# Pacing the modulation sums of a two-layer diffusion trunk by two running clocks instead of fixed rates

## The chip, the cores and the metric

The kernel runs on one core of one Trainium2 chip. The time is device microseconds (us) of that core for one execution, the median of several runs. The engines are TensorE (PE; its weight loads are listed apart as PEld), VectorE (DVE), ScalarE (ACT), GpSimd (POOL) and SyncE (SP), which here only issues DMAs.

## What is computed

Two transformer layers, for 128 context rows and 256 latent rows that share all weights. Each layer starts from an adaLN modulation, one row vector for the context and one for the latents:

```
def _adaln(cond, w_mod, b_mod):
    m = jax.nn.silu(cond) @ w_mod + b_mod
    return jnp.split(m, 3, axis=-1)          # shift, scale, gate
h = _rmsnorm(y, norm_g) * (1.0 + scale) + shift
y = y + gate * mixer(h @ w_in) @ w_out
```

Layer 0's mixer is a gated linear recurrence (HGRN2) beside a grouped-query attention; layer 1's is a windowed attention. `w_mod` is 2048 x 6144 in each layer, all in float32. The change touches only when the parts of `silu(cond) @ w_mod` that are needed later are computed.

## The kernel before

**The matrix work.** All 384 rows stay on the chip. The large products (`h @ w_in`, `@ w_out`) run on PE in the fp32r type with three products each: a weight tile `raw` is split by ACT into `whi` (L328) and by DVE into the difference `wlo` (L330), and the activations stand split as `hh`, `hl`. `group` (L333) makes 512 columns of one product in eight **steps** of two 128-row weight tiles (512 KB): a step is 18 matmuls of 512 columns when rows are the output's partitions, or 24 of 384 columns when weights are. A group holds three or four of four PSUM buffers; the next group can take a buffer only after it was read out.

**The start stage.** Shift and scale of layer 0 are needed at once; `start_mod` makes them on PE while `start_group` (L688 to L690) multiplies the first six groups with the rows of the activations that are ready. It has 54 steps. I number the steps of the whole kernel 0 to 269: 0 to 53 are the start stage, then 27 groups of eight follow, 54 to 93 for the recurrence's value and the attention's inputs, 94 to 125 for gates, 126 to 157 for layer 0's output projection (four groups), 158 to 237 for layer 1's inputs, 238 to 269 for its output projection.

**The later sums.** Eight parts of the modulation are made beside that: four of layer 1's shift and scale (`mod_part`, in the order 16, 24, 0, 8) and four pairs of gate blocks (`mod_gates`: for layer 0's output groups 0 and 1, then 2 and 3; the same for layer 1). Each part reads 16 tiles of 512 KB, `mraw`, from the SP queue (L231) and sums them on DVE in `mod_acc`: two instructions of 1024 elements per tile (L244 for the first tile, L246 for the other fifteen). There is one `acc` buffer. A `mod_part` ends with matmuls against ones on PE (L256), a `mod_gates` with a split (ACT L285, DVE L287), matmuls against ones (L288, L289) and an addition of the bias (DVE L290); these free `acc` for the next part. `finish((layer, g))` after an output group makes the rest of the sum that its gate needs; the read-out of the group's PSUM (L1047) multiplies by that gate, so it waits for it.

**The order.** Each part is a Python generator, cut at its `yield`s into units: one that issues the first loads, sixteen of one tile each, and the ends. `step()` (L84) advances the recurrence and the attention by one piece; then `pump()` (L308) adds the rate `pace[1]` to a credit and calls `unit()` once for each whole credit. A piece that yields a weight takes `WEIGHT` times that from the credit (L90). Rates are 0.6 units per step in the start stage, 1.3 up to step 117, 0.9 up to 157, then 0.6. Where code stands sets its priority; the framework's scheduler places instructions on the engines by priority and readiness as it estimates them, so an instruction of low priority can come out earlier than its place in the code. The pieces of weights carry a raised priority (`tc.high_priority(BOOST)`).

Of the kernel before, what the change touches and what calls it, by code (L numbers as in the profile page):

```python
# [8 lines left out]
F32R = mybir.dt.float32r  # L9
# [5 lines left out]
P = 128  # L15
# [3 lines left out]
EPS = 1e-6  # L19
NEG = -1e30  # L20
BOOST = 100000
RATE = 1.3
RATE0 = 0.6
RAWB = 4
HIB = 3
# [3 lines left out]
PB = 2  # L29
EVY = 1  # L30
SRAW = 3
RATE1 = 0.9
WEIGHT = 0.25
RATE2 = 0.6
RATE3 = 0.6
MRAWB = 3
# [6 lines left out]

@with_exitstack
def trunk_kernel(ctx: ExitStack, tc: tile.TileContext, I, O):
    nc = tc.nc
    PSUM = bass.MemoryType.PSUM

    cpool = ctx.enter_context(tc.tile_pool(name="cpool", bufs=1))
# [27 lines left out]
    queue, due, pace = [], [], [0.0, 0.0]  # L77
# [6 lines left out]
    def step():  # L84
        if due:
            for f in due.pop(0):
                f()
        while queue:
            try:
                pace[0] -= WEIGHT * (next(queue[0]) or 0)  # L90
                return
            except StopIteration:
                queue.pop(0)
# [204 lines left out]
    def unit():  # L298
        while now or rows or mods:
            if not now:  # L300
                now.append((rows or mods).pop(0))
            try:
                next(now[0])
                return
            except StopIteration:
                now.pop()

    def pump():  # L308
        pace[0] += pace[1]
        while pace[0] >= 1.0:  # L310
            unit()
            pace[0] -= 1.0

# [62 lines left out]
    def group_a(w, c0, hq, after=None):  # L376
        return group(w, c0, hq, True, after)
# [266 lines left out]
    for g in range(4):  # L644
        x = xs[g]
# [24 lines left out]
    def pairs(k0, k1):  # L670

        out = []
        while k0 < k1:
            out.append((k0, min(2, k1 - k0, 4 - k0 % 4)))
            k0 += out[-1][1]
        return out
# [61 lines left out]
    for i, (k0, k1) in enumerate(phases):  # L738
# [4 lines left out]
        n = len(first) * len(pairs(k0, k1))  # L743
# [159 lines left out]

    pace[1] = RATE
    queue.append(hgrn_prep(0))
# [68 lines left out]
    def gate_heads(ps, o):  # L974
        gs = []
        for h in range(4):
            G = mpool.tile([P, 512], F32, tag="t2", bufs=T2B, name=nm("gt"))[:, 0:T]
            gate_fm(ps[h][:, 0:T], G)
            nc.vector.tensor_tensor(out=o[:, h], in0=o[:, h], in1=G, op=ALU.mult)
# [10 lines left out]
    ready0[0] = True  # L990
    pace[1] = RATE1
    gate_heads(group_a(W0, 7168, h0, after0), oB[1])
# [35 lines left out]
    for i, (c0, n) in enumerate(COLS):  # L1028
        g, o = c0 // 512, c0 % 512
        last = i == len(COLS) - 1  # L1030
        if o == 0:
            x = load_x("CD"[g % 2], g, nc.gpsimd)
# [102 lines left out]
    for c0, n in COLS:  # L1135
# [9 lines left out]
        for b in range(3):  # L1145
            for h in range(0, n, half):
                y = y4[:, b, o + h:o + h + half]
                t = mpool.tile([P, 512], F32, tag="t2", bufs=T2B, name=nm("t2"))[:, 0:half]
# [62 lines left out]
```

## Time and profile before

| | |
|---|---|
| median of 3 runs | 1369.67 us (1367.2 to 1371.61) |
| the profiled execution | 1371.0 us, of which the span from first to last instruction is 1369.1 us |
| mean granted TensorE clock | 0.994 |
| PE, PEld busy | 97%, 82% |
| DVE, ACT, POOL busy | 74%, 47%, 6% |

The busy share of DVE is uneven: in 40 slices of the span it is between 4 and 9 tenths. The profile is read by stages: which engine a stage waits for, and for how long PE stands still in it.

### The profile page before, as it was taken

How to read it: one execution, taken by the hardware profiler on the slowest of the kernel's cores; microseconds unless marked ns; L12 is line 12 of the kernel's file. 1: busy time of each engine (PE TensorE's matmuls, PEld its weight loads, DVE VectorE, ACT ScalarE, POOL GpSimd, SP SyncE). 2: the span in 40 equal slices, each digit the busy share in tenths (PEclk: the TensorE clock that was granted, in tenths of full speed). 3: DMA queues.
4: the chain of work that ended last, by engine and by line, in shares of the span. 5: the costliest groups of instructions: out<-in, count | busy, mean ns of one | idle time of the engine just before them, and what ended most of it. 6: DMA issues, size and time to landing. Idle time of an engine off the chain costs nothing.

```text
span 1369.1 us, 19104 instructions
## 1 busy us (share of the span) xinstructions
PE 1325.7 (97%) x7093; PEld 1126.7 (82%) x7093; DVE 1016.5 (74%) x1602; ACT 650.0 (47%) x1299; POOL 76.9 (6%) x84
## 2 busy tenths in 40 slices
PE   5899998999999999999999999999999999999998
PEld 4677777997888888688987787888888999998877
DVE  6588557998996799699498658994656664489734
ACT  3532233477554534566443336444766763352221
POOL 1000000000010022010000000200000101000000
PEclk9999999999999999999999999999999999999999
DMA  9999898745653367468458744784332335457642
GB/s 280 302 336 329 273 300 293 245 131 184 209 174 119 108 204 225 156 216 260 139 182 282 243 143 133 221 293 124 93 93 78 103 118 166 132 174 249 220 146 77
DMA packets 138317, 265.42 MB, mean 194 GB/s; under 512 B 8944, under 2 KB 46768, under 8 KB 138224
## 3 DMA queue, kind: packets, MB, share of 16 engines
q1 hardware_dynamic: 132592, 246.52, 55.6%
q0 software_dynamic: 5376, 17.60, 4.4%
q8 instruction: 56, 0.92, 0.3%
q14 instruction: 37, 0.30, 0.1%
q10 hardware_dynamic: 256, 0.08, 0.0%
HBM read 256.04 MB, written 8.13 MB: 193 GB/s over the span
## 4 chain that ended last, share of the span: by engine, by line
PE 70%; DVE 6%; ACT 1%; issue 1%; DMA 1%; POOL 0%; DVEq 0%; POOLq 0%
PE mm L354 59%; PE px L546 3%; DVE acc L246 2%; DVE wlo L330 2%; PE px L606 1%; PE px L623 1%; PE px L569 1%; PE px L861 1%; DMA mraw<-in_l_w_mod_dram 1%; PE px L864 1%; PE px L536 0%; PE px L878 0%; PE px L396 0%; PE px L868 0%; PE px L894 0%
## 5 line engine op out<-in xcount | busy, mean ns | idle before, releaser
L328 ACT CAST whi<-raw 128x1024 fp32r<-128x1024 f32 (+1 forms) x270 | 278.3, 1032 | 516.9 <-PE mm L354 394.6
L330 DVE TENSOR_TENSOR wlo<-raw,whi 128x1024 fp32r<-128x1024 f32 (+1 forms) x270 | 322.8, 1196 | 207.7 <-PE mm L354 161.2
L354 PE MATMUL mm<-whi,hh 128*128 128x512 f32 x1008 | 399.4, 397 | 2.0 <-DVE tF L639 1.7
L354 PE MATMUL mm<-wlo,hh 128*128 128x512 f32 x1008 | 391.6, 391 | 2.8 <-DVE wlo L330 2.8
L354 PE MATMUL mm<-whi,hl 128*128 128x512 f32 x1008 | 393.4, 391 | 0.6 <-DVE hl L1023 0.4
L246 DVE SCALAR_TENSOR_TENSOR acc<-mraw,csil,acc 128x1024 f32<-128x1024 f32 x240 | 299.4, 1277 | 13.0 <-DMA mraw<-in_l_w_mod_dram 13.0
L354 PEld LDWEIGHTS mm<-whi,hh 128*128 128x128 f32 x1008 | 189.4, 188 | 42.7 <-DVE tF L639 2.1
L354 PEld LDWEIGHTS mm<-wlo,hh 128*128 128x128 f32 x1008 | 189.3, 188 | 42.7 <-DVE wlo L330 5.6
L354 PEld LDWEIGHTS mm<-whi,hl 128*128 128x128 f32 x1008 | 189.3, 188 | 41.0 <-DVE hl L1023 0.8
L688 PE MATMUL mm<-hh,whi 128*128 128x384 f32 x384 | 132.9, 352 | 11.6 <-ACT whi L328 5.7
L354 PE MATMUL mm<-hh,whi 128*128 128x384 f32 x384 | 131.4, 342 | 0.0
L689 PE MATMUL mm<-hl,whi 128*128 128x384 f32 x384 | 131.2, 342 | 0.1
L354 PE MATMUL mm<-hh,wlo 128*128 128x384 f32 x384 | 129.3, 337 | 0.0
L354 PE MATMUL mm<-hl,whi 128*128 128x384 f32 x384 | 128.9, 336 | 0.0
L690 PE MATMUL mm<-hh,wlo 128*128 128x384 f32 x384 | 125.5, 341 | 2.2 <-DVE wlo L330 2.1
L688 PEld LDWEIGHTS mm<-hh,whi 128*128 128x128 f32 x384 | 73.6, 193 | 26.4 <-ACT whi L328 8.7
L690 PEld LDWEIGHTS mm<-hh,wlo 128*128 128x128 f32 x384 | 72.8, 191 | 5.4 <-DVE wlo L330 4.1
L689 PEld LDWEIGHTS mm<-hl,whi 128*128 128x128 f32 x384 | 73.7, 192 | 0.9 <-DVE hl L430 0.4
L354 PEld LDWEIGHTS mm<-hh,whi 128*128 128x128 f32 x384 | 72.1, 188 | 1.5 <-DVE tM L639 0.5
L354 PEld LDWEIGHTS mm<-hl,whi 128*128 128x128 f32 x384 | 72.2, 188 | 0.9
L354 PEld LDWEIGHTS mm<-hh,wlo 128*128 128x128 f32 x384 | 72.1, 188 | 0.6 <-issue 0.2
L581 ACT ACTIVATE p<-px,nb,rs 128x384 f32<-128x384 f32 (+1 forms) x72 | 42.4, 595 | 11.9 <-DVE nb L579 8.2
(450 smaller groups left out, 1395.7 us busy)
## 6 DMA issues: line engine op xcount, KB each, us to landing
raw<-in_l_w_in_dram SPq DMA_DIRECT2D x194, 512.0 KB, 3.9
mraw<-in_l_w_mod_dram SPq DMA_DIRECT2D x192, 512.0 KB, 5.1
raw<-in_l_w_out_dram SPq DMA_DIRECT2D x64, 512.0 KB, 4.5
raw<-in_l_w_in_dram SPq DMA_DIRECT2D x12, 256.0 KB, 7.4
tK<-in_l_b_mod_dram POOLq DMA_DIRECT2D x6, 256.0 KB, 6.0
y1d<-tA POOLq DMA_DIRECT2D x2, 768.0 KB, 7.3
tD<-y1d POOLq DMA_DIRECT2D x2, 768.0 KB, 6.5
tL<-y1d POOLq DMA_DIRECT2D x2, 768.0 KB, 6.5
```

The lines of the kernel that those rows point to most:

```text
L246: nc.vector.scalar_tensor_tensor(out=acc[:, c], in0=raw, scalar=s, in1=acc[:, c], op0=ALU.mult, op1=ALU.add)
L328: nc.scalar.copy(hi, raw)
L330: nc.vector.tensor_tensor(out=lo, in0=raw, in1=hi.bitcast(F32), op=ALU.subtract)
L354: nc.tensor.matmul(ps[c], lhsT=a, rhs=b, start=(kt == 0 and i == 0), stop=(kt + nk == KT and i == len(ops) - 1))
L546: nc.tensor.matmul(out, lhsT=a, rhs=b, start=(i == 0), stop=(i == len(ops) - 1))
L569: nc.tensor.matmul(s[:, 0:n], lhsT=qT[b][:, hc], rhs=kT[:, g, 0:n], start=True, stop=True)
L581: nc.scalar.activation(p[:, j], ss[j], AF.Exp, bias=nb[:, j:j + 1], scale=rs[:, i + j:i + j + 1], accum_out=sm[:, j:j + 1])
L606: nc.tensor.transpose(pp[:, k * P:k * P + P], p[:, j, k * P:k * P + P], ident)
L623: nc.tensor.matmul(o, lhsT=vs[kb][:, gc], rhs=ptt[0][:, j], start=(j == 0), stop=(j == len(ks) - 1))
L688: nc.tensor.matmul(ps[c][:, 0:T], lhsT=wh, rhs=hh[:, kq], start=(kt + k == k0), stop=False)
L689: nc.tensor.matmul(ps[c][:, 0:T], lhsT=wh, rhs=hl[:, kq], start=False, stop=False)
L690: nc.tensor.matmul(ps[c][:, 0:T], lhsT=wl, rhs=hh[:, kq], start=False, stop=(kt + k == k1 - 1))
```

## The change

The tracing code gets two clocks, in estimated us: `t` grows with each instruction that is issued to TensorE, `v` with each to VectorE, by three formulas. They exist only while the program is traced; on the chip no instruction is added or removed. `pump()` now makes a unit only where the credit allows it and `v` plus 2.7 is not above `t`; before that, `v` is raised to at least `t` minus 6. The credit is capped, the rates 1.3 and 0.9 become 2.0, the rates of the start stage and of layer 1 stay 0.6, and the weights that the pieces yield are no longer used.

```
-RATE = 1.3
+RATE = 2.0
-RATE1 = 0.9
-WEIGHT = 0.25
+RATE1 = 2.0
+BANK = 6.0
+UNIT = 2.7
...
+    clock = {"t": 0.0, "v": 0.0}
...
+    def cost_t(name, out, *a, lhsT=None, rhs=None, **k):
+        if rhs is None:
+            return 0.11
+        if lhsT.dtype == F32R:
+            return 0.013 + free(rhs) / 2400
+        return 4 * free(rhs) / 2400 * free(lhsT) / P
+
+    def cost_v(name, *a, **k):
+        aps = [x for x in (*a, *k.values()) if hasattr(x, "shape")]
+        n = max(free(x) for x in aps[:2])
+        return 0.12 + n / 1900 if name in ("tensor_copy", "tensor_scalar", "memset") else 0.17 + n / 950
...
             try:
-                pace[0] -= WEIGHT * (next(queue[0]) or 0)
+                next(queue[0])
                 return
...
     def pump():
-        pace[0] += pace[1]
-        while pace[0] >= 1.0:
+
+        pace[0] = min(pace[0] + pace[1], 2.0 + pace[1])
+        clock["v"] = max(clock["v"], clock["t"] - BANK)
+        while pace[0] >= 1.0 and clock["v"] + UNIT <= clock["t"]:
             unit()
             pace[0] -= 1.0
```

What is left out is a wrapper, `Counted`, that adds the cost to the clock and passes each call on to the engine, and `free`, the number of elements of one partition.

## Rows read from the trace of the kernel before

**Rows 1.** The page's part 1: busy us, share of the span, instructions.

```profile
PE 1325.7 (97%) x7093; PEld 1126.7 (82%) x7093; DVE 1016.5 (74%) x1602; ACT 650.0 (47%) x1299; POOL 76.9 (6%) x84
```

**Rows 2.** Windows: us, busy PE, PEld, DVE, ACT, POOL (x instructions), clock, DMA share, GB/s.

```profile
0.00:40.00 40.00, 25.02 (x187) 19.47 (x187) 23.96 (x54) 18.68 (x47) 3.59 (x10) 0.91 0.94 293
...
768.00:800.00 32.00, 32.00 (x142) 25.89 (x141) 13.70 (x16) 10.31 (x14) 0.00 (x0) 1.00 0.56 181
...
1240.00:1280.00 40.00, 40.00 (x179) 33.11 (x178) 39.50 (x37) 10.56 (x10) 0.75 (x1) 1.00 0.86 288
```

**Rows 3.** Groups by line, DVE: busy us, mean ns, idle before and its releasers.

```profile
L330 DVE TENSOR_TENSOR wlo<-raw,whi 128x1024 fp32r<-128x1024 f32 (+1 forms) x270 | 322.8, 1196 | 207.7 <-PE mm L354 161.2 <-ACT whi L328 22.4 <-issue 19.5
L246 DVE SCALAR_TENSOR_TENSOR acc<-mraw,csil,acc 128x1024 f32<-128x1024 f32 x240 | 299.4, 1277 | 13.0 <-DMA mraw<-in_l_w_mod_dram 13.0
```

**Rows 4.** Windows of line L256 alone, the ones matmuls: PE and PEld busy.

```profile
180.00:190.00 10.00, 1.04 (x8) 0.26 (x8) 1.00 1.03 352
315.00:325.00 10.00, 1.06 (x8) 0.16 (x8) 1.00 0.31 103
475.00:485.00 10.00, 1.06 (x8) 0.16 (x8) 1.00 0.24 68
575.00:585.00 10.00, 1.07 (x8) 0.16 (x8) 1.00 0.40 105
```

**Rows 5.** Windows of line L289 alone, the gates' second matmul against ones.

```profile
690.00:700.00 10.00, 1.23 (x3) 0.56 (x3) 1.00 0.37 119
```

**Rows 6.** Windows of line L246 alone, the sums: DVE busy us and instructions.

```profile
480.00:550.00 70.00, 34.19 (x28) 1.00 0.72 219
...
839.00:920.00 81.00, 36.93 (x30) 1.00 0.70 227
920.00:1200.00 280.00, 0.00 (x0) 1.00 0.39 115
```

**Rows 7.** All engines' windows in the start stage.

```profile
205.00:210.00 5.00, 5.00 (x40) 4.17 (x39) 1.35 (x2) 1.05 (x1) 0.00 (x0) 1.00 0.97 341
...
225.00:230.00 5.00, 5.00 (x21) 5.00 (x20) 3.99 (x4) 1.51 (x2) 0.00 (x0) 0.65 0.70 222
230.00:235.00 5.00, 5.00 (x31) 5.00 (x30) 3.99 (x6) 1.46 (x2) 0.00 (x0) 1.00 0.90 320
```

**Rows 8.** Timeline of SP, 185 to 211 us: start, us, issue (first and last).

```profile
185.00 0.50 SPq L231 DMA_DIRECT2D mraw<-in_l_w_mod_dram  x1
...
210.83 0.46 SPq L231 DMA_DIRECT2D mraw<-in_l_w_mod_dram  x1
```

**Rows 9.** Timeline of ACT and PE at 223 us, [idle before <-releaser].

```profile
223.07 1.04 ACT L328 CAST whi<-raw 128x1024 fp32r<-128x1024 f32 x1 [3.75 <-DMA raw<-in_l_w_in_dram]
224.17 0.69 PE L688 MATMUL mm<-hh,whi 128*128 128x384 f32 x1 [4.77 <-ACT whi L328]
```

**Rows 10.** Timeline of PE at 553 us.

```profile
553.14 0.50 PE L354 MATMUL mm<-whi,hh 128*128 128x512 f32 x1 [1.66 <-DVE tF L639]
```

**Rows 11.** Timeline of DVE and PE, 739 to 742 us.

```profile
739.55 1.28 DVE L246 SCALAR_TENSOR_TENSOR acc<-mraw,csil,acc 128x1024 f32<-128x1024 f32 x1 [4.99 <-DMA mraw<-in_l_w_mod_dram]
...
742.03 0.50 PE L354 MATMUL mm<-wlo,hh 128*128 128x512 f32 x1 [2.08 <-DVE wlo L330]
```

**Rows 12.** Timeline of DVE in layer 0's output projection.

```profile
700.41 0.75 DVE L244 TENSOR_SCALAR acc<-mraw,csil 128x1024 f32<-128x1024 f32 x1
...
722.09 0.69 DVE L1047 TENSOR_TENSOR tA<-mm,tK 128x512 f32<-128x512 f32 x1
...
727.37 4.86 DVE L246 SCALAR_TENSOR_TENSOR acc<-mraw,csil,acc 128x1024 f32<-128x1024 f32 x4
...
766.66 1.27 DVE L246 SCALAR_TENSOR_TENSOR acc<-mraw,csil,acc 128x1024 f32<-128x1024 f32 x1
...
796.64 0.68 DVE L1047 TENSOR_TENSOR tA<-mm,tK 128x512 f32<-128x512 f32 x1
...
800.32 0.68 DVE L287 TENSOR_TENSOR alo<-acc,ahi 128x512 fp32r<-128x512 f32 x1
```

More of the change, by code (lines that the diff above doesn't have):

```diff
@@ L45, in trunk_kernel, with free, __init__, __getattr__ @@
 def trunk_kernel(ctx: ExitStack, tc: tile.TileContext, I, O):
-    nc = tc.nc
+    clock = {"t": 0.0, "v": 0.0}
+    def free(ap):
+        n = 1
+        for d in ap.shape[1:]:
+            n *= d
+        return n
+    def cost_t(name, out, *a, lhsT=None, rhs=None, **k):
[8 more added lines that the diff above has]
+        return 0.12 + n / 1900 if name in ("tensor_copy", "tensor_scalar", "memset") else 0.17 + n / 950
+    class Counted:
+        def __init__(self, engine, key, cost):
+            self.engine, self.key, self.cost = engine, key, cost
+        def __getattr__(self, name):
+            f = getattr(self.engine, name)
+            def counted(*a, **k):
+                clock[self.key] += self.cost(name, *a, **k)
+                return f(*a, **k)
+            return counted
+    class Core:
+        vector, tensor = Counted(tc.nc.vector, "v", cost_v), Counted(tc.nc.tensor, "t", cost_t)
+        def __getattr__(self, name):
+            return getattr(tc.nc, name)
+    nc = Core()
     PSUM = bass.MemoryType.PSUM
```

## The prediction

> **What bounds the kernel now.** Part 1 of the page comes first: PE is busy for 1325.7 us of the span of 1369.1, DVE for 74% [rows 1]. Only 43.4 us have no matmul in flight, 15 of them in the first 40 us [rows 2], among the first loads and transposes, and the windows then show whether a busy PE still hides anything. In 1240 to 1280 us, with PE busy throughout, 179 matmuls of 512 columns run, one per 0.223 us [rows 2]; nothing in the change makes these faster. So a change that only moves DVE work can win no more than what PE stands still or crawls. The question is where PE waits for DVE, or for a DMA that a sum's load held up, and whether the change moves a sum away from there.
>
> The weight loads say something else at first sight: PEld is busy only 82% of the span [rows 1]. The Trainium skill ("Perfetto Trace Analysis", section "Identifying the Most-Contended Engine") holds that matmul busy time tells little about headroom and that weight-load busy time is the measure; by it 1369.1 - 1126.7 = 242 us would be open. But in the window without a wait PEld stands at 33.11 of 40 us, 83% [rows 2], so 82% is about what a full PE shows here, and the trace disagrees with the rule.
>
> I read three places where a sum costs PE time. In the start stage PE stands for 4.77 us at 224 us, because ACT's cast waited 3.75 us for a weight tile's DMA [rows 9], and the clock falls: in 225 to 230 us it is 0.65 of full speed and 21 matmuls run where 31 run in the next 5 us [rows 7]; the missing ten cost 10 x 5.00/31 = 1.6 us. (A mean of 0.65 of 2.4 GHz is 1.2 GHz for some 70% of the 5 us.) At 553 us PE waits 1.66 us for DVE's gate product [rows 10], in a stretch where the sums take 34.19 of 70 us of DVE [rows 6]. At 742 us PE waits 2.08 us for a difference that stood behind a sum which itself waited 4.99 us for its tile [rows 11]. Together 4.77 + 1.6 + 1.66 + 2.08 = 10.1 us, and that is nearly all that better placing can win outside the first 200 us.
>
> **What the change does to the order.** No instruction is added or removed; what moves are the units' places, and each unit takes along its two DVE instructions, one load on SP's queue, and at a part's end the PE, ACT and POOL work. Where they go follows from the diff's formulas. A step of 18 wide matmuls adds 18 x (0.013 + 512/2400) = 4.07 to `t`, a step of 24 narrow ones 4.15; a difference adds 0.17 + 1024/950 = 1.25 to `v`, a unit twice that, 2.50. The trace has 1.196 and 2 x 1.277 for these [rows 3], so the clocks are close for this work. In a step with nothing else on DVE a unit therefore fits (3.75 against 4.07), in most steps of the recurrence, whose own DVE work is 4 to 6, none does. I carried both clocks through the 270 steps, adding up what the code issues in each. Tiles summed, before and after: 16 and 16 at step 30, 28 and 26 at step 53, 48 and 37 at step 87, 73 and 65 at step 117, 80 and 79 at step 133, 93 and 94 at step 149, 96 each at 150. In layer 1 the third pair's tiles lie in steps 178 to 203 instead of 180 to 229; the last pair stays within one step.
>
> These are places in the code, not times. The trace shows how loosely the two hang together: layer 1's first gate sum has its tiles spread over steps 180 to 229 before, the middle of layer 1, but 30 of its L246 run in 839 to 920 us and none in the 280 us after [rows 6]. The scheduler lets sums run as soon as `acc` is free and DVE has room. What holds a sum back is the end of the sum before it, since there is one `acc`, and those ends lie on PE, whose queue is always full: the four groups of ones matmuls run at about 185, 320, 480 and 580 us [rows 4], where their code stands (steps 31, 59, 88, 107), and the first gate pair's at 690 to 700 us (step 126) [rows 5]. So the moves that count are those of the ends: step 31 to 33, 59 to 60, **88 to 103, 107 to 116, 126 to 134**, while the second gate pair (150) and layer 1's pairs (231 to 230, 261 to 260) stay. In time, by interpolating between those rows: 28 steps take 320 - 185 = 135 us, so two steps are 10 us; 19 steps take 100 us, so 15 are 79 and the third end comes at 559 us; 19 steps take 115, so the fourth comes at about 634; the fifth at the end of the first output group, 722 us [rows 12].
>
> **Part by part.** *The start stage, 185 to 230 us.* The second part's two first loads go from step 33 to 35 and its first tiles from 35 to 37. Before, four of its loads of 512 KB are issued from 185.00 to 210.83 us, among the weights [rows 8]; about 10 us later, two of them fall behind the tile that PE waits for. At the 341 GB/s of that stretch [rows 7] a load takes 0.524 MB / 341 GB/s = 1.5 us of the DMAs, so the late tile comes up to 3.1 us earlier. If that shortens the stop enough, the slow clock's 1.6 us goes too. Bounds: nothing won, because the tile's issue and not its transport was late, and everything, 4.77 + 1.6 = 6.4 us; a loss is possible, since the loads now meet other weights, and no more than one load's 1.5 us twice. I take -3.0, the transport alone, which is the nearest row. What comes after the cast in that place is the pace of the matmuls.
>
> *480 to 560 us.* The fourth part's sum starts only at 559 us instead of 480. DVE has 28 x 1.22 = 34 us less to do in 480 to 550 us [rows 6] and the wait at 553 us (1.66) should go, with a few tenths of smaller ones. The sum then runs over 559 to about 630 us, in place of the first gate pair's, which ran there before: the load of DVE in 560 to 640 us stays what it was. I take -2.0, bounds -3.3 (the wait's size twice, for the smaller ones) and +1.0 (a new such wait of a little more than the old).
>
> *The gate of output groups 0 and 1.* Its last tile and its end are short by two units at step 133, so `finish` makes them after group 0's matmuls, where before they were done at step 126, 30 us ahead. The read-out of group 0 stands behind this: ACT split, DVE difference, two matmuls, addition. The same already happens with the second pair, at step 150: group 2's first read-out starts at 796.64 us and `acc` is read for the last time at 800.32 + 0.68 [rows 12], and PE is busy for all of 768 to 800 us [rows 2]. I cost it at nothing: the tiles before the last are long summed, PE has one free PSUM buffer, and cast weights for two steps stand ready; if that cover fails, it costs the 4.4 us from 796.64 to 801.0.
>
> *The gate of output groups 2 and 3.* Its sum can start only when the first pair has left `acc`, 4 to 5 us after group 0's read-out begins, so at about 728 us, not 700.41. It needs two first tiles and 30 x 1.2 (four take 4.86 us [rows 12]), some 37.5 us, and beside it DVE has nine of the twelve block operations of two read-outs at 0.69 [rows 12], 6.2 us; a difference of 1.2 per step of 4.08 leaves 0.71 of DVE, so 44 / 0.71 = 62 us, to 790 us. It is wanted at 794 to 796 us. Before it ended at 766.66 + 1.27 = 767.9, 27 us ahead; now some 5 us are left, less a split. A single late tile like the 4.99 us at 739.55 [rows 11] uses that up. Bounds 0 and +8; I take +1.5. The stop of 2.08 us at 742 us itself belongs to this sum: it moves 28 us on, its load meets other transfers, and it may come again. Bounds -2.1 and 0; I take -1.2.
>
> *Layer 1.* The third pair's sum starts when `acc` is free and ran at 839 to 920 us [rows 6], far ahead of its code; its new places are earlier still. Nothing waits for it until step 230. Zero, bounds -1 and +1. *The rest* (sums within the first 185 us come 1 to 3 tiles later, then catch up at step 30) I leave at nothing, bounds -2 and +2, since SP's queue shifts by single loads there.
>
> **The sum.** -3.0 - 2.0 + 1.5 - 1.2 = -4.7 us. Against the profiled execution's own 1371.0 us that gives 1366.3; that execution lies 1.3 us above the median, so against 1369.67 us it is **1365.0 us**.
>
> **The rivals.** *The scheduler undoes it.* Since sums run up to 280 us ahead of their code, the ends that move might bring only the same waits at other places. For it speaks that DVE's total and every deadline stay; against it, that three ends move by 29 to 79 us. It gives 1369 us, between 1366 and 1372.
>
> *DVE is late at the third output group.* One mechanism: the first gate pair forced at step 134 pushes the second pair's sum to 728 us, and if it ends after 794 us, group 2's read-out waits, three of four PSUM buffers stay full and PE stops. The point from which it decides is DVE's share: at 0.71 free it ends at 790 us; with one wait of 5 us for a tile and at 0.65 free it ends at 728 + 5 + 68 = 801, the first read-out comes near 804 instead of 796.64, and PE loses some 7 us less what its free buffer covers, with the wins elsewhere halved: 1369.7 - 2.5 + 6 = 1373 us, up to 1377. For it speaks that DVE has been full in such stretches (39.50 of 40 [rows 2]); against it, that such a full stretch shows PE busy throughout.
>
> *All three places go.* The start stage runs through without the stop and the slow clock (-6.4), the places at 553 and 742 us too (-3.3 and -2.1), and the third group is in time: 1369.7 - 11.8 = 1357.9 us, from 1355 to 1361.5. The rule of the skill named above would call for still more, as it sees 242 us open; no row bears that out, so it adds nothing to this case's chance.
>
> **How the numbers follow.** About 0.3%, 4.1 us, is what a measurement of this kernel tells from no change. The forecast's case (1361.5 to 1367.5) has 0.45, of which 0.27 lie below 1365.6; the undoing scheduler 0.25, all but 0.02 within; late gates 0.14; all three places 0.16. Faster: 0.27 + 0.16 = 0.43. Within: 0.18 + 0.23 = 0.41. Slower: 0.14 + 0.02 = 0.16. The range 1356 to 1375 leaves out the ends of the second and the third rival, about 0.12.
>
> **What would show it.** L256 in windows about 195, 325, 560 and 635 us and the first L289 at about 722 us: the ends moved as counted. The gap before L688 at about 220 us below 3 us, and the clock in the 5 us after it at 1.00. L246 nearly absent in 490 to 550 us, with no PE gap at 553. The second pair's last L246 before 795 us; if it is later and L1047 of group 2 starts after 800 us with PE idle before, the second rival holds. If the ends lie where I say and the three stops are still there, the first rival holds. If the ends lie elsewhere, my count of the clocks is wrong, and with it the whole sum.

## The result, and the profile after

The changed kernel takes **1355.79 us** (median of 4 runs, 1353.84 to 1356.77) beside 1369.83 us for the kernel before (4 runs on the same chip): ratio 0.9897, 95% interval 0.9878 to 0.9917. That is 14 us where I forecast 4.7, and 0.2 us below the low end of my range. The case "all three places go" (1357.9 us) came closest in time, though not by its own terms.

Part 1 of the page of the changed kernel (span 1355.0 us, in answer to [rows 1]):

```profile
PE 1321.0 (97%) x7093; PEld 1125.7 (83%) x7093; DVE 1019.0 (75%) x1602; ACT 647.9 (48%) x1297; POOL 72.4 (5%) x84
```

PE's busy time falls by 4.7 us, so the other 9.4 us of the 14.1 are time in which PE had no matmul in flight; PE's instructions are as many as before and DVE's work is the same but for its placing. ACT has 1297 instructions instead of 1299 [rows 1], so "no instruction is added or removed" does not hold to the last one: the two are table loads (`ACT_TABLE_LOAD`, 1.28 us each), 9 before and 7 after. The other 1290 are the same in number, and how many table loads stand among them goes with their order; the kernels below have between 5 and 15.

The weight loads' share is hardly moved: the rule of the Trainium skill that I weighed ("Perfetto Trace Analysis", section "Identifying the Most-Contended Engine") would still call 1355.0 - 1125.7 = 229 us open, while in 756 to 790 us, PE without a wait, PEld stands at 27.08 of 34 us (row below). The page names a second measure beside it, the share of the peak rate that the matmuls' arithmetic reaches, which I did not compare.

To see where the time went I set the start of the n-th of the 5328 matmuls of the large products in one trace beside the same in the other. The lead of the changed kernel:

| stretch of before, us | lead won | what it is |
|---|---|---|
| 0 to 218 | 0.2 | between 1.9 behind and 2.9 ahead on the way |
| **218 to 238** | **7.0** | the stop at 224 us and the slow clock after it |
| **277 to 366** | **3.7** | four small waits and what hangs on them |
| 470 to 654 | 0.3 | the wait at 553 us goes, others come |
| 654 to 811 | 0.9 | the stop at 742 us is smaller |
| 811 to 1309 | -0.1 | layer 1 |
| **1309 to 1348** | **2.2** | the last gate |

Sum 14.2; the spans differ by 14.1.

Each row compares one execution with one other, and the profiled execution of the kernel before is one of its longer ones: 1371.0 us, where its medians beside the experiments are 1367.0 to 1368.5. Two kernels of the experiments have its order on every engine until far behind the start stage (to 331 us in "all but the first two sums", to 1198 us in "only layer 1's gates"). Their stops at the same matmul (timelines of PE):

```profile
221.35 0.69 PE L696 MATMUL mm<-hh,whi 128*128 128x384 f32 x1 [3.42 <-ACT whi L336]
...
224.92 0.69 PE L696 MATMUL mm<-hh,whi 128*128 128x384 f32 x1 [3.86 <-ACT whi L336]
```

Against these two the row of 7.0 us would be 6.3 and 5.5, and the three traces of one order lie up to 2.3 us apart at 238 us. So a difference of one or two us between single traces of the start stage says little. The 3.7 us are steadier: 0.0 in "only layer 1's gates", which keeps the old order there, and 3.7 in the changed kernel as in two that share its order in most of that stretch (the first two sums alone, ends in different steps).

All of the changed kernel's PE and DVE instructions have the line of the wrapper, L77, so its rows are read by tiles. Windows of its engines (columns as in [rows 2]):

```profile
210.00:215.00 5.00, 3.32 (x30) 2.17 (x29) 3.76 (x10) 1.89 (x3) 0.00 (x0) 1.00 0.94 346
215.00:220.00 5.00, 5.00 (x30) 5.00 (x30) 3.52 (x4) 3.19 (x6) 0.00 (x0) 1.00 1.02 370
...
269.00:283.00 14.00, 14.00 (x82) 14.00 (x82) 13.91 (x15) 11.63 (x15) 0.00 (x0) 1.00 0.59 177
297.00:320.00 23.00, 23.00 (x104) 19.02 (x103) 17.58 (x33) 17.26 (x23) 0.00 (x0) 1.00 0.50 159
332.00:356.00 24.00, 24.00 (x133) 20.40 (x132) 23.20 (x36) 12.81 (x25) 1.43 (x2) 1.00 0.63 201
...
756.00:790.00 34.00, 34.00 (x150) 27.08 (x149) 32.81 (x33) 10.83 (x14) 0.58 (x1) 1.00 0.86 296
```

The first two answer [rows 7]: of the 4.77 us stop some 1.7 us are left, and the clock is at 1.00 behind it, where before it was at 0.65. Rows three to five are the stretches of the 3.7 us: PE has no idle time in them. In the kernel before it had four waits there, the first four of these rows; the other three are the last gate's (timeline of PE):

```profile
281.25 0.44 PE L690 MATMUL mm<-hh,wlo 128*128 128x384 f32 x1 [0.40 <-DVE wlo L330]
...
286.90 0.44 PE L688 MATMUL mm<-hh,whi 128*128 128x384 f32 x1 [0.28 <-DVE tK L696]
...
325.05 0.66 PE L265 MATMUL px<-ct,ev 128*128 128x128 f32 x4 [0.69 <-ACT ev L260]
...
364.32 0.49 PE L898 MATMUL px<-s,q 128*128 128x128 f32 x2 [0.61 <-DVE s L885]
...
1332.48 0.49 PE L288 MATMUL px<-ahi,ones_r 128*128 128x512 f32 x1 [0.20 <-ACT ahi L285]
1333.66 0.50 PE L289 MATMUL px<-alo,ones_r 128*128 128x512 f32 x1 [0.69 <-DVE alo L287]
1334.45 0.50 PE L354 MATMUL mm<-whi,hh 128*128 128x512 f32 x1 [0.29 <-DVE t L1149]
```

The ends of the four sums for layer 1's shift and scale (windows of PE on tile `acc`, busy us and instructions, in answer to [rows 4]):

```profile
190.00:200.00 10.00, 1.04 (x8) 1.00 0.90 280
318.00:328.00 10.00, 1.07 (x8) 1.00 0.49 148
550.00:560.00 10.00, 1.07 (x8) 1.00 0.52 153
630.00:640.00 10.00, 1.06 (x8) 1.00 0.66 217
```

They lie at 195, 323, 553 and 635 us; I had said 195, 325, 560 and 635. The first gate pair's end, which I had put at about 722 us, comes at 709 (timeline of PE), which is the lead of 13 us at that point:

```profile
708.89 0.40 PE L77 MATMUL px<-alo,ones_r 128*128 128x512 f32 x1
```

The new waits (timelines of PE and of DVE):

```profile
213.16 0.66 PE L77 MATMUL px<-ct,ev 128*128 128x128 f32 x4 [0.71 <-ACT ev L756]
214.79 0.44 PE L77 MATMUL mm<-hh,whi 128*128 128x384 f32 x1 [0.98 <-ACT whi L370]
...
501.42 0.50 PE L77 MATMUL mm<-wlo,hh 128*128 128x512 f32 x1 [1.39 <-DVE wlo L77]
...
636.92 0.66 PE L77 MATMUL px<-ct,ev 128*128 128x128 f32 x4 [0.71 <-ACT ev L300]
...
734.50 0.50 PE L77 MATMUL mm<-wlo,hh 128*128 128x512 f32 x1 [1.50 <-DVE wlo L77]
```

```profile
497.80 1.76 DVE L77 TENSOR_TENSOR tG<-tG,sm 128x1536 f32<-128x1536 f32 x1 [4.98 <-POOL sm L444]
...
500.15 1.22 DVE L77 TENSOR_TENSOR wlo<-raw,whi 128x1024 fp32r<-128x1024 f32 x1
...
732.03 1.29 DVE L77 SCALAR_TENSOR_TENSOR acc<-mraw,csil,acc 128x1024 f32<-128x1024 f32 x1 [4.11 <-DMA mraw<-in_l_w_mod_dram]
733.23 1.22 DVE L77 TENSOR_TENSOR wlo<-raw,whi 128x1024 fp32r<-128x1024 f32 x1
```

### The profile page after: what moved, and what is told of

It is laid out like the page before. It is cut to its first block, busy times and chain, and to the rows that moved or that the text cites. A ratio compares the mean times of both kernels' runs of the same rounds, so it can differ in the third digit from the quotient of the medians.

```text
span 1355.0 us, 19101 instructions
## 1 busy us (share of the span) xinstructions
PE 1321.0 (97%) x7093; PEld 1125.7 (83%) x7093; DVE 1019.0 (75%) x1602; ACT 647.9 (48%) x1297; POOL 72.4 (5%) x84
## 4 chain that ended last, share of the span: by engine, by line
PE 91%; DMA 4%; DVE 3%; ACT 1%; POOL 1%; issue 0%; DVEq 0%; ACTq 0%; SPq 0%; POOLq 0%
PE mm L77 77%; PE px L77 14%; DMA raw<-in_l_w_in_dram 2%; DMA mraw<-in_l_w_mod_dram 1%; DVE wlo L77 1%; DVE acc L77 1%; DMA tB<-in_x_sample_dram 0%; ACT whi L370 0%; POOL sm L444 0%; DVE tB L77 0%; DMA rowc<-in_c_dram 0%; DVE tG L77 0%; ACT tE L469 0%; DVE tH L77 0%; POOL r L444 0%
## 5 line engine op out<-in xcount | busy, mean ns | idle before, releaser
L77 DVE TENSOR_TENSOR wlo<-raw,whi 128x1024 fp32r<-128x1024 f32 (+1 forms) x270 | 323.4, 1198 | 188.0 <-PE mm L77 148.6
L77 PE MATMUL mm<-whi,hh 128*128 128x512 f32 x1008 | 398.9, 396 | 0.0
L77 PE MATMUL mm<-wlo,hh 128*128 128x512 f32 x1008 | 391.7, 391 | 3.2 <-DVE wlo L77 3.2
L77 PE MATMUL mm<-whi,hl 128*128 128x512 f32 x1008 | 393.5, 391 | 0.6 <-DVE hl L77 0.6
L77 DVE SCALAR_TENSOR_TENSOR acc<-mraw,csil,acc 128x1024 f32<-128x1024 f32 x240 | 299.0, 1279 | 9.0 <-DMA mraw<-in_l_w_mod_dram 9.0
L77 PE MATMUL mm<-hh,whi 128*128 128x384 f32 x768 | 264.4, 347 | 7.1 <-ACT hh L471 4.6
L77 PE MATMUL mm<-hl,whi 128*128 128x384 f32 x768 | 259.2, 338 | 0.0
L77 PE MATMUL mm<-hh,wlo 128*128 128x384 f32 x768 | 254.5, 338 | 0.2 <-DVE wlo L77 0.2
L77 PEld LDWEIGHTS mm<-wlo,hh 128*128 128x128 f32 x1008 | 189.3, 188 | 42.7 <-DVE wlo L77 5.8
L77 PEld LDWEIGHTS mm<-whi,hl 128*128 128x128 f32 x1008 | 189.3, 188 | 40.8 <-DVE hl L77 1.5
L77 PEld LDWEIGHTS mm<-whi,hh 128*128 128x128 f32 x1008 | 189.4, 188 | 39.3 <-ACT tE L824 0.8
L77 PEld LDWEIGHTS mm<-hh,whi 128*128 128x128 f32 x768 | 145.3, 190 | 22.2 <-issue 10.1
L77 PEld LDWEIGHTS mm<-hh,wlo 128*128 128x128 f32 x768 | 144.8, 189 | 2.7 <-DVE wlo L77 1.0
L77 PEld LDWEIGHTS mm<-hl,whi 128*128 128x128 f32 x768 | 145.5, 190 | 1.2 <-issue 0.2
L623 ACT ACTIVATE p<-px,nb,rs 128x384 f32<-128x384 f32 (+1 forms) x72 | 42.4, 596 | 15.0 <-DVE nb L77 14.5
L77 PE MATMUL px<-mraw,cs 128*32 128x256 f32 (+1 forms) x576 | 40.4, 377 | 4.9 <-DMA mraw<-in_l_w_mod_dram 4.9
L633 ACT ACTIVATE p<-p,sum 128x384 f32<-128x384 f32 (+1 forms) x72 | 36.1, 540 | 15.1 <-DVE sum L77 13.2
L77 DVE TENSOR_REDUCE mx<-px 128x1 f32<-128x384 f32 (+1 forms) x54 | 29.7, 567 | 9.3 <-PE px L77 8.9
L77 PEld LDWEIGHTS px<-mraw,cs 128*32 128x32 f32 x576 | 16.3, 114 | 20.0 <-issue 8.2
L77 PEld LDWEIGHTS px<-ct,p 128*128 128x128 f32 x168 | 20.1, 141 | 8.3 <-issue 2.8
L444 POOL TENSOR_TENSOR rs<-rs,nhalf 128x12 f32<-128x12 f32 x6 | 14.7, 2450 | 227.5 <-DVE rs L77 227.5
```

Source lines behind the costliest of these rows:

```text
L77: return f(*a, **k)
L444: nc.gpsimd.tensor_tensor(out=out, in0=out, in1=nhalf[:, 0:out.shape[1]], op=ALU.pow)
L623: nc.scalar.activation(p[:, j], ss[j], AF.Exp, bias=nb[:, j:j + 1], scale=rs[:, i + j:i + j + 1], accum_out=sm[:, j:j + 1])
L633: nc.scalar.activation(p[:, j], p[:, j], AF.Copy, scale=sm[:, j:j + 1])
```

## The experiments

To move units alone, `pump` is replaced by a written list with one digit per step, the number of units (rows of 54 digits, steps 0 to 269). Filled with the numbers that I counted for a kernel, the list gives that kernel's order: in the traces "only layer 1's gates" has the order of the kernel before on every engine up to 1198 us, and "ends in different steps" that of the changed kernel up to 636 us, each to where its own move begins. So the count of the clocks was right; from there single sums can be moved.

```diff
     def pump():
-        pace[0] += pace[1]
-        while pace[0] >= 1.0:
+        for _ in range(int(PLAN[at[0]])):
             unit()
-            pace[0] -= 1.0
+        at[0] += 1
```

Theory 1: the gain is the start stage's, because fewer loads of sums stand in SP's queue ahead of the tile that PE waits for. Theory 2 (my prediction's): it is spread over the places at 224, 553 and 742 us. Theory 3: it comes from the running clocks as such.

### Which sums carry the gain

**Only the first two sums** at the changed kernel's places (rows 0 and 1 of the list, from before's):

```diff
- "010101101011010110101101011010110101101011010110101101"
- "011121120011010110101110101011010111112111111102011111"
+ "001101101010000200010200111011101011010110101101011010"
+ "010112150011010110101110101011010111112111111102011111"
```

> Units placed from a written list, one number per step: the first two sums (parts 16 and 24) at the places of the changed kernel, all others at the places of the kernel before. By the traces the changed kernel gained 7.0 us between 218 and 231 us, where the start stage's stop was, and 3.7 us more by 365 us. Theory (the start stage's gain comes from the first two sums' later places): 1369.8 - 7 = 1363 us, ratio 0.995, and if the 3.7 us too come from sum two's later end, 1359 us. Rival (the scheduler's order as a whole changed, and no part of the list alone gives the gain): 1367 to 1372 us.

Measured: 1360.18 us, 0.9945 (0.9930 to 0.9961). The trace wins 7.0 us at the stop and 3.7 us to 366 us, and loses 0.7 net behind it: 0.9 are won up to 811 us and 1.6 lost at the last gate, where the clock falls (last section).

**All but the first two** (from after's list):

```diff
- "001101101010000200010200111011101011010110101101011010"
- "010112140000010010000010000010000011121100101002004210"
+ "010101101011010110101101011010110101101011010110101101"
+ "011121020000010010000010000010000011121100101002004210"
```

> The complement: parts 16 and 24 at the places of the kernel before, all other units at those of the changed kernel. Theory: the stop of about 4.8 us near 224 us with its slow clock stays, the gains behind 280 us come, 1369.8 - 7 = 1363 us if all of them belong to sums three to eight, 1366 us if the 3.7 us belong to sum two. Rival (no part alone gives a gain): 1367 to 1372 us.

Measured: 1363.36 us, 0.9969 (0.9956 to 0.9981). A stop of 3.42 us at 221.35 us stays, and of the 3.7 us its trace wins 1.0. The two ratios multiply to 0.9914; the whole change is 0.9897, so the two halves add up within their intervals.

**Only layer 1's gates** (rows 3 and 4):

```diff
- "000000000000000001100001000000100001000000100000010010"
- "101101011010110101101011010110101101011010110100000000"
+ "000000000000000110101101011001110101011011000000000000"
+ "000000000000001011010100120101011010110101101000000000"
```

> Only layer 1's two gate sums at the places of the changed kernel: the last sum's end in step 260 instead of 261, the one before in 230 instead of 231. Theory (2.2 us of the gain lie at 1316 to 1340 us, where the last gate's matmuls against ones stood in the way of PE before and do not after): ratio 0.9984, 1367.6 us, and no gap at L288 and L289 near 1333 us. Rival (that gain came with the other moves): ratio 1.000, the gaps of 0.47, 0.94 and 0.56 us are still there.

Measured: 1364.54 us, 0.9981 (0.9968 to 0.9994); in the trace 2.2 us are won at the end and the rest stays. The one unit that moves from step 261 to 260 is worth that: the last gate's chain of ACT, DVE and PE then runs between matmuls of one more step, as the timeline of PE in the changed kernel shows, where before PE had nothing else to do (1332 to 1335 us above):

```profile
1316.52 0.41 PE L77 MATMUL px<-ahi,ones_r 128*128 128x512 f32 x1
1316.77 0.39 PE L77 MATMUL mm<-wlo,hh 128*128 128x512 f32 x1
...
1317.46 0.40 PE L77 MATMUL mm<-wlo,hh 128*128 128x512 f32 x1
1317.69 0.41 PE L77 MATMUL px<-alo,ones_r 128*128 128x512 f32 x1
```

**Only the second sum:**

```diff
- "010101101011010110101101011010110101101011010110101101"
- "011121120011010110101110101011010111112111111102011111"
+ "010101101011010110101101011010110001010110101101011010"
+ "010112150011010110101110101011010111112111111102011111"
```

> Only the second sum (part 24) at the places of the changed kernel: its first loads two steps later than before, in step 35, first tile in step 37; sum one keeps its places of before. Theory (two loads of the second sum fewer ahead of the weight tile that PE waits for at 224 us): the stop there shrinks from 4.8 us to below 2 us, the clock stays at 1.00, 1363 us or less. Rival (sum one's tiles, one to three steps later over steps 11 to 30, changed the whole backlog of transfers): the stop stays, 1367 to 1372 us.

Measured: 1359.64 us, 0.9942 (0.9925 to 0.9958), as much as both sums together. The windows of all engines show no stop and no slow clock:

```profile
215.00:220.00 5.00, 5.00 (x31) 5.00 (x30) 2.67 (x4) 2.47 (x3) 0.00 (x0) 1.00 1.03 390
220.00:225.00 5.00, 5.00 (x31) 5.00 (x30) 4.69 (x7) 2.11 (x2) 0.00 (x0) 1.00 1.00 365
```

How the tile comes earlier is seen on SP and ACT. SP issues in order, and the weights of the next stage stand in its queue among those of the start stage; their buffers are still in use by `start_mod` on PE, so SP stands for them (waits of SP's queue in 200 to 217 us, before: total us, times, longest):

```profile
SPq L326 <- PE px L709: 7.6, 2, 4.8
```

In the kernel before the awaited tile is issued right behind the second of these waits, at 215.12 us (first row below), and its cast, ACT's 38th of a weight, starts at 223.07 us [rows 9]. With the second sum two steps later one more weight of the start stage goes out ahead of the first wait, and the 38th cast is the second of these rows (timeline of ACT in this kernel):

```profile
207.26 1.05 ACT L336 CAST whi<-raw 128x1024 fp32r<-128x1024 f32 x1 [10.68 <-DMA raw<-in_l_w_in_dram]
208.56 1.06 ACT L336 CAST whi<-raw 128x1024 fp32r<-128x1024 f32 x1 [0.25 <-PE mm L698]
```

That is 14.5 us earlier, 10.5 of them beyond the 4.0 by which this trace is ahead at that point anyhow (matmul 740 of the count above).

The changed kernel itself gets only half of this. Its 38th tile is issued between the two waits of SP, which end at 206.28 and 212.06 us, and is cast 6.7 us earlier than before (timelines of SP before, of SP and of ACT in the changed kernel):

```profile
215.12 0.46 SPq L326 DMA_DIRECT2D raw<-in_l_w_in_dram  x1
...
208.50 0.42 SPq L368 DMA_DIRECT2D raw<-in_l_w_in_dram  x1
...
216.42 1.03 ACT L370 CAST whi<-raw 128x1024 fp32r<-128x1024 f32 x1
```

There the 37th tile also falls behind the first wait, and the stop that is left, 0.98 us, is for this one. All fourteen traces line up by the place of the 38th tile:

| its issue | kernels | stop of PE for a weight tile there |
|---|---|---|
| behind both waits | before, all but the first two, layer 1's gates, first loads, late and spread out | 2.74 to 4.77 us |
| between them | changed, first two, ends apart, late begin, late and fewer | 0.98 to 1.71 us |
| ahead of both | second sum, second sum on POOL's queue, rate 0.5, fewer tiles | none |

So a sum's load costs not only its transport but a place: the tile that gives way falls behind one or two waits of SP.

### What in the start stage does it

**Before's places, the second sum's loads on POOL's queue:**

```diff
-            nc.sync.dma_start(raws[kt], I[f"l{l}_w_mod"][kt * P:kt * P + P, c0:c0 + 1024])
+            eng = nc.gpsimd if (l, c0) == (1, 24 * P) else nc.sync
+            eng.dma_start(raws[kt], I[f"l{l}_w_mod"][kt * P:kt * P + P, c0:c0 + 1024])
```

> Units at the places of the kernel before; the sixteen loads of the second sum (part 24) are issued on POOL's queue instead of SP's, in the same places. The same bytes cross the same DMA engines. Theory A (transport: two loads' 3.1 us of transfer stood ahead of the awaited weight tile): the stop near 224 us stays at 3 to 5 us and the time at 1367 to 1370 us. Theory B (order of issue: SP's queue works its issues off in order, and each sum load that stands in it holds back the weight loads behind it, so that one fewer weight tile is under way): the stop falls below 2 us, and 1361 to 1363 us, less what POOL's own issues cost.

Measured: 1368.51 us, 0.9987 (0.9971 to 1.0002). The weight tile is no longer waited for at 224 us, but a stop comes earlier, for the tiles of `start_mod`, whose transfers share the DMAs: the last two land 6.8 and 9.2 us behind their issue (5.1 and 6.1 before). And 8.2 us are lost at 299 to 319 us (timelines of PE and, last, of DVE):

```profile
214.79 0.79 PE L726 MATMUL px<-ct,ev 128*128 128x128 f32 x4 [1.93 <-ACT ev L723]
...
314.24 0.80 PE L363 MATMUL mm<-wlo,hh 128*128 128x512 f32 x1 [3.70 <-DVE wlo L339]
...
309.36 0.56 DVE L838 TENSOR_TENSOR hg<-hg 128x384 f32<-128x384 f32 x1 [3.19 <-ACT hg L830]
```

No sum is waited for there: the second sum's last load goes out at 248.84 us and its last tile is summed at 261.9. DVE waits for the recurrence's own work on ACT, twice for over 3.1 us, and ACT has nine table loads in 285 to 330 us where the kernel before has four. So the awaited weight does depend on its place in SP's queue, as theory B has it, and moving the loads to another queue brought a stop for other tiles and a worse order of the recurrence; the time is theory A's, for a reason that it did not name.

**Only the second sum's first loads** two steps later:

```diff
- "010101101011010110101101011010110101101011010110101101"
+ "010101101011010110101101011010110002101011010110101101"
```

> Units at the places of the kernel before, except that the one unit which issues the second sum's first two loads stands in step 35 instead of 33, where its first tile stands. Theory (the places of these two loads among the weights of the start stage decide): most of the 8.9 us that the run with the whole second sum moved won, 1361 to 1363 us. Rival (all of the second sum's tiles, two steps later each, are needed): the stop near 224 us stays above 3 us, 1366 to 1369 us.

Measured: 1366.99 us, 0.9991 (0.9977 to 1.0005), not to be told from no change, which is the rival's time. In the trace, one of the fastest of its ten executions (1365.62 us), the stop shrinks to 2.74 us and the clock stays at 1.00, 4.0 us less there (timeline of PE, then windows):

```profile
219.90 0.44 PE L696 MATMUL mm<-hh,whi 128*128 128x384 f32 x1 [2.74 <-ACT whi L336]
```

```profile
215.00:220.00 5.00, 2.26 (x14) 1.94 (x12) 3.18 (x4) 3.49 (x6) 0.00 (x0) 1.00 1.05 404
220.00:225.00 5.00, 5.00 (x29) 5.00 (x30) 4.87 (x5) 2.11 (x2) 0.00 (x0) 1.00 0.88 290
```

The awaited tile is still issued behind SP's second wait (212.75 us; its cast starts at 218.80). So the transports alone are worth at most 4.0 us with the clock, 2.4 and 3.2 against the two other traces of the old order, and the ten executions show 1.2 us (between 0.7 lost and 3.1 won). How the 7.0 us divide is not settled to a us; the greater part by the times needs the place.

**The kernel before with one constant changed,** no clocks:

```diff
-RATE0 = 0.6
+RATE0 = 0.5
```

> The kernel before with its fixed rate of later sums' tiles per step at 0.5 instead of 0.6: 23 tiles by step 53, the second sum's first loads in step 39, ends of the sums in steps 35, 64, 92 and 112. Theory (what the change brings comes from fewer tiles ahead of the awaited start tile, whatever rule places them): the stop of 4.9 us at 224 us goes, 1357 to 1361 us. Rival (it takes the running clocks, since an even rate meets other waits of VectorE behind 280 us): 1364 to 1370 us.

Measured: 1359.75 us, 0.9943 (0.9923 to 0.9963). Theory 1 for the greater part: a fixed rate gives over half of the gain. This interval and the changed kernel's do not overlap; the rest lies in places behind 366 us, which the clocks choose better than this rate (by the traces 5.6 us). The stop at 224 us is gone, 7.8 us are won by 244 us and 11.4 by 366 us. From 470 to 646 us 3.4 us of it are lost again, in waits like these (timeline of PE), the last of them the one of 553 us, ahead of which sums still stand in this kernel; and at 771 us PE waits 1.69 us more behind a sum whose tile is late by 3.66 us:

```profile
507.02 0.50 PE L354 MATMUL mm<-wlo,hh 128*128 128x512 f32 x1 [1.65 <-DVE wlo L330]
...
545.19 0.50 PE L354 MATMUL mm<-whi,hh 128*128 128x512 f32 x1 [1.55 <-DVE tF L639]
```

### What is left in the changed kernel

**Sum four's two ends in different steps** (117 and 118; from after's list):

```diff
- "220111212412020111001111110002211101111211000000000000"
+ "220111212142020111001111110002211101111211000000000000"
```

> Units at the places of the changed kernel, except that the fourth sum's two ends (ones matmuls, then the transposes that read what ACT copied from them) stand in steps 117 and 118 instead of both in 117. In the changed kernel PE lost 0.43 + 1.29 + 0.40 us there (635 to 640 us). Theory: the 1.29 and 0.40 go, 1354 us, ratio to the kernel before 0.9885. Rival: the wait is for DVE work that moves along, 1355 to 1356 us.

Measured: 1355.67 us, 0.9899 (0.9876 to 0.9923). By the distance between the starts of its matmuls the stop at 636 us shrinks from 1.30 to 0.66 us, and the time does not follow by an amount that can be told. The next four kernels keep this edit; their diffs are against its list.

**Sum one begins in step 12 instead of 2:**

```diff
- "001101101010000200010200111011101011010110101101011010"
+ "000000000000111111111110111011101011010110101101011010"
```

> As the run with the ends apart, and the first sum begins in step 12 instead of 2, with one tile a step until it has caught up in step 24. Before and after, PE stops for 4.84 us at 58 us with a slow clock behind it, and two of the first sum's DVE instructions stand among the work that it waits for. Theory (those instructions and loads lengthen the stop): 2 to 5 us less, 1349 to 1352 us, and the stop below 3 us. Rival (the stop is the chain of transposes, modulation and cast itself): the stop stays at 4.8 us; 1353 to 1356 us.

Measured: 1355.46 us, 0.9899 (0.9873 to 0.9925). By the same measure the stop at 58 us, 4.85 us in the changed kernel, becomes 2.65; the trace is 4.4 us ahead of its parent's at 89 us and 1.7 us behind at 219.

**Fewer tiles in the start stage,** sum two from step 41 instead of 35, 22 tiles there instead of 26:

```diff
- "001101101010000200010200111011101011010110101101011010"
- "010112140000010010000010000010000011121100101002004210"
+ "001101101010000200010200111011101010000001010101010101"
+ "010112110011011111110010000010000011121100101002004210"
```

> The changed kernel's order with sum one at its places (steps 2 to 34) and sum two from step 41 (ends 68 and 69): 22 tiles ahead of the start stage's end instead of 26, without the late begin. Theory (bytes on the one queue bound the start stage): some 1352 to 1355 us, faster than the changed kernel. Rival (no transfer is waited for any more ahead of 230 us, or the tiles put off cost the same later): 1355 to 1357 us.

Measured: **1352.05 us**, 0.9879 (0.9842 to 0.9916). PE has no wait left between 210 and 235 us (windows):

```profile
210.00:215.00 5.00, 5.00 (x40) 4.42 (x31) 1.93 (x6) 3.03 (x6) 0.00 (x0) 1.00 1.00 360
215.00:220.00 5.00, 5.00 (x30) 5.00 (x30) 2.09 (x2) 2.61 (x4) 0.00 (x0) 1.00 0.65 224
```

Its trace is 3.7 us ahead of the changed kernel's at 228 us and 4.2 at the end; 1.8 us of this are there by 157 us, where the two orders are still the same, so some 1.9 belong to the move. It is the fastest here, by 3.7 us of median; but it stood beside a kernel before of 1367.04 us, so by the ratios it is 2.5 us, and the two intervals overlap. That it is faster than the changed kernel is not shown.

**Both, late and fewer:**

```diff
- "001101101010000200010200111011101011010110101101011010"
- "010112140000010010000010000010000011121100101002004210"
+ "000000000000111011010110110101101101010111010101010101"
+ "010112110011011111110010000010000011121100101002004210"
```

> The changed kernel's order, except that sum one begins in step 12 (one tile every 1.6 steps, ends in steps 39 and 40) and sum two only in step 41 (ends 68 and 69), so 22 of the sums' tiles fall ahead of the start stage's end instead of 26. Theory (the start stage is bound by the bytes that its one in-order queue brings; a tile is 512 KB and about 1.5 us): four tiles fewer are about 6 us at most, of which those that the later steps give back are lost; time 1349 to 1352 us, ratio about 0.986, and the lead over the kernel before is still there behind 230 us. Rival (the tiles that are put off cost the same between 300 and 420 us, where VectorE and the queue have no more room than here): 1354 to 1357 us, the same as the changed kernel.

Measured: 1354.1 us, 0.9893 (0.9862 to 0.9925). Beside the kernel with fewer tiles alone, the late begin leads by 5.1 us at 157 us, by 0.9 at 214 us, after waits for a tile of `start_mod` and a weight, and is 1.1 behind at the end. That the lead would be kept has fallen.

**Late, and spread out further,** 20 tiles in the start stage, sum two's ends in steps 75 and 76:

```diff
- "001101101010000200010200111011101011010110101101011010"
- "010112140000010010000010000010000011121100101002004210"
+ "000000000000111010101010110101010101011010011010110110"
+ "101101101011011010100111111110000011121100101002004210"
```

> The changed kernel's order with sum one from step 12 on, a tile every 1.85 steps (ends in steps 43 and 44), and sum two from step 46 on, a tile every 1.6 steps (ends 75 and 76), sum three from step 77; 20 of the sums' tiles fall ahead of the start stage's end instead of 26, and everything from step 88 on stays at the changed kernel's places. Theory (every load ahead of an awaited start tile costs its transport, early and late in the start stage, and later steps have room for the tiles): the lead of 5 to 6 us that the late begin brings by 90 us is kept this time, because sum two's loads come behind the awaited tiles; 1347 to 1351 us, ratio about 0.985. Rival (the start stage's weights alone fill the queue, so the early lead is lost again by 220 us, as it was where sum one began late with the other sums unchanged): 1352 to 1356 us. Third case (sum two's tiles and ends meet the recurrence's own VectorE work at 280 to 400 us): 1355 us or more, with waits for VectorE there.

Measured: 1362.51 us, 0.9963 (0.9946 to 0.9980). A miss, the third case in its time: the lead is 10 us at 190 us, then come a stop for a weight tile and one in the recurrence (timeline of PE):

```profile
207.87 0.56 PE L696 MATMUL mm<-hh,whi 128*128 128x384 f32 x1 [3.51 <-ACT whi L336]
...
352.91 0.80 PE L906 MATMUL px<-s,q 128*128 128x128 f32 x2 [4.81 <-DVE s L893]
```

At the second, DVE is not full of sums: none runs in 346 to 354 us, and DVE waits 2.58 us for ACT's `hg`, which stands behind a table load of 1.28 us on ACT. ACT has seven table loads in 330 to 370 us, where the kernels before and after have one. Moving sums has moved the order of the recurrence's own work, as where POOL issued the loads; why the scheduler took this order stays open.

## Why the prediction was wrong, point by point

**The order was right.** Every unit's step, and the ends of the four sums of [rows 4] within 7 us.

**The start stage: the term was mis-sized.** I took -3.0, "the transport alone", with -6.4 as the bound; measured 7.0 between the two traces, 5.5 and 6.3 against the other two traces of the old order. The step that failed is the choice of the lower row: I argued that two loads of 1.5 us are two transports. The runs show two parts: the transports alone (first loads moved) give at most 4.0 us with the slow clock in a trace, and 1.2 by the times; the rest is the tile's place in SP's queue, in the changed kernel ahead of the second wait for PE instead of behind it. I had listed SP's issues [rows 8], but not its waits. And "the late tile's issue was late" stood in my text as the reason why nothing would be won; it was late because of the loads ahead. The second sum alone does it all, its first two loads alone do not.

**277 to 366 us: not in the sum.** 3.7 us in a stretch that I left out, since no wait of it was over 0.7 us. Four waits of together 1.98 us were there, and I read only the long ones. The first two sums bring it (3.7 in the kernel that moves only them; 1.4 with the second sum alone). The same stretches before (windows):

```profile
278.00:292.00 14.00, 13.32 (x74) 12.42 (x73) 13.70 (x14) 11.45 (x15) 0.00 (x0) 1.00 0.29 94
306.00:330.00 24.00, 23.30 (x107) 17.82 (x105) 17.91 (x24) 22.00 (x30) 0.00 (x0) 1.00 0.46 141
342.00:368.00 26.00, 25.39 (x137) 21.27 (x137) 26.00 (x38) 12.72 (x25) 1.44 (x2) 1.00 0.68 219
```

In the first, DVE was no less loaded after (13.91 of 14 us), so there it is the order and not the amount. In the second ACT is emptier after (17.26 of 23 us for 22.00 of 24), with one table load in 285 to 330 us for four; in the third it is DVE (23.20 of 24 us for all of 26). The table loads alone are not the reason: the kernel at rate 0.5 has three there and wins 3.6 us in 277 to 366 us, the second sum alone has one and wins 1.4. What it is stays open: the first 1.5 us of it also went where only the queue of the second sum's loads was changed, and stayed where only the second sum was moved.

**480 to 640 us: right mechanism, wrong sum.** The wait at 553 us went, with the sums that stood ahead of it. I took -2.0; measured -0.3, within my bounds. What took its place was a new wait at 501 us: DVE takes `tG` next and stands 4.98 us for POOL's power, and the weight's difference queues behind it. In the kernel before, sums ran on DVE in that time. With the sums gone (none is left on DVE in 480 to 500 and 501 to 553 us, as forecast) a waiting instruction stood in front: the sums had been cover, and I costed their going as pure gain. Other traces bear this out: `tG` waits 5.01 and 4.99 us in "all but the first two sums" and at rate 0.5, where no sum stands ahead of it either, and not at all with the first two sums or the second alone, where sums run up to it as before. The two ends of sum four in one step added 0.6 us at 636 us.

**The gates of layer 0.** The stop of 742 us came again, 1.50 us for 2.08 [rows 11], once more behind a sum that waits for its tile (4.11 us for 4.99). I took -1.2 and the trace has -0.9 for the whole output projection. The loss of +1.5 at the third group did not come: the second pair's last tile was summed at 780.5 us, where my 790 is 778 once the lead of 12 us is taken off, and the first read-out of group 2 starts at 784.62 us, 12.0 us ahead of 796.64 [rows 12], so nothing was late. The margin was as thin as I had it, and it held; I had priced an expected loss where the working said "in time". PE is busy for all of 756 to 790 us. The rival of late gates falls. The first pair's late end, costed at nothing, cost nothing: PE is busy for all of 708 to 724 us.

**Layer 1: half right.** The third pair's move cost nothing, as I said. But "the last pair stays within one step" was costed at nothing without a row read for it, and that one step is worth 2.2 us, more than the places at 553 and 742 us gave together. The last gate is the one with no work behind it; I should have read its chain in the trace of before.

In sum: of the 9.4 us that the forecast missed, 4.0 are the start stage, 3.7 the small waits, 2.2 the last gate and 1.5 the third group that did not come, less 1.7 at 480 to 640 us and about 0.3 elsewhere. The rival "the scheduler undoes it" held for 480 to 640 us alone.

## What to carry to other kernels

In an in-order queue a load of low priority costs more than its transport where it pushes an urgent load behind one that waits for a buffer: read the queue's own waits and ask which side of them the awaited tile is on. Low-priority work on an engine is also cover: before booking its removal as gain, look what would be first in the queue then, and for whom it waits. And read the last chain before the end and the many small waits as well as the three long ones; here they made 5.9 of 14 us.

## What was not expected of the hardware

The clock does not follow from the length of the stop alone. After the 4.77 us of the kernel before it was 0.65 in the next 5 us [rows 7]; after 2.74 us in the kernel with the first loads moved it was 1.00; but where sum one began late, two waits of 0.71 and 1.21 us in 212 to 214 us were followed by this window (all engines):

```profile
215.00:220.00 5.00, 5.00 (x21) 5.00 (x20) 3.47 (x4) 2.56 (x5) 0.00 (x0) 0.66 1.02 366
```

The changed kernel has two waits of 0.71 and 0.98 us at nearly the same place, and 1.00 behind them; with the first two sums alone they are 0.71 and 1.71 us, longer than in the row above, and the clock stays at 1.00. The last gate shows it too: the kernel before has waits of 0.20, 0.69 and 0.29 us there and 1.00 behind them; with the first two sums alone they are 0.20, 0.68 and 0.30 us, and the trace loses 1.6 us there (windows of all engines, before and with the first two sums):

```profile
1330.00:1340.00 10.00, 8.82 (x35) 6.22 (x35) 8.08 (x12) 2.22 (x3) 0.00 (x0) 1.00 0.34 125
...
1320.00:1330.00 10.00, 8.82 (x29) 6.13 (x28) 7.07 (x11) 1.67 (x2) 0.00 (x0) 0.83 0.23 88
```

What tells these apart no run here shows.
